# Biased attention on one core: a first group of four head pairs instead of three, bf16 loads by GpSimd, V landed in place, and the odd slot of the two-chunk pass read in two exps

## The chip, the cores and the metric

The kernel runs on one core of one Trainium2 chip. The metric is the device time of one execution in microseconds, lower is better. The engines are named as in the profile: PE (matmuls, with PEld for its weight loads), DVE (VectorE), ACT (ScalarE), POOL (GpSimd) and SP (SyncE). DMAs that SP and ACT issue go over hardware queues (q1 and q10 in the profile); DMAs that POOL issues go over the software queue q0, and these can cast f32 to bf16 on the way.

## The reference

```python
def setup_inputs():
    batch, n_heads, seq_len, head_dim = 4, 8, 1024, 64
    # q, k, v: (4, 8, 1024, 64) float32, 0.1 * normal; bias: (1, 1, 1024, 1024) float32, 0.1 * normal

def reference(q, k, v, bias):
    scale = 1.0 / np.sqrt(head_dim)
    scores = scale * np.matmul(q, k.transpose(0, 1, 3, 2)) + bias
    scores_max = np.max(scores, axis=-1, keepdims=True)
    attn = np.exp(scores - scores_max) / (np.sum(np.exp(scores - scores_max), axis=-1, keepdims=True) + 1e-8)
    return np.matmul(attn, v).astype(np.float32)
```

## The kernel before

**Tiling.** The 32 heads are taken as 16 pairs. A head's 1024 queries are 8 chunks of 128, and so are its keys. Scores are made transposed, keys on partitions, in two PSUM tiles `sx` and `sy` of three banks each (a bank is 512 f32 columns); the even "slots" use `sx`, the odd ones `sy`. The query chunks are split into three passes, `CH = {"A": (6, 2), "B": (3, 3), "C": (0, 3)}`: pass A takes chunks 6 and 7 (two banks a slot), B and C three chunks each (three banks a slot). One step is a pass, a pair and a head h, and it is two slots.

**The bias.** It is added once at the beginning of a pass, by matmuls of the bias chunk with a scaled identity (a "restart"). After that PSUM is never cleared: each step adds this head's scores and subtracts those of the head before it in the same 128-row contraction. That is what the operand tiles are for: `KA`, `KB`, `QA`, `QB` hold the two heads of a pair on the two halves of the partitions, with signs, and the lower half of `KB` and `QB` at pair r + 1 is a copy of pair r. They are rings of `RP = 9` pairs.

**Exp and AV.** ACT reads a slot with one exp (or two, where `cut_of` says so) into the bf16 ring `E` of `EB = 56` banks. Some slots leave their last bank to DVE, which makes the exp in a chain of seven instructions (`d_fixed`, `d_steps`, lines 222 to 241). The AV matmuls (`av_blocks`, line 272) take 128x128 blocks of `E` as weights and V with a column of ones, `VV` (pairs x 16 chunks x 65), as the moving operand; `evac` divides by the sum and stores.

**Transposes and copies.** Raw k and q (bf16, `kr` and `qr`) are transposed by PE (`transpose_pe`, line 147) into the PSUM tiles `xa` and `xb`, which the AV accumulators use as well. DVE copies them to `KA` and `QA`; from pair 3 on the second copies are made by DMAs on SP (lines 724, 727, 748, 752).

**Groups and order.** The pairs go in three groups, `range(0, 3)` with passes ABC, `range(3, 8)` with CAB, `range(8, 16)` with BCA, so a pass is restarted seven times. The first six slots are written out by hand (lines 288 to 482). From there a planner written in Python puts the instructions in order when the kernel is built: it holds a time for each engine (`t_act`, `t_pe`, `t_dve`), the costs `EXP`, `EXP0` and others, due times of the first loads (`raw_at`, `v_at`, `R["bias", ...]`), and picks the next fill (`pe_fill`), transposing piece (`pe_piece`), AV block (`pe_av`) or early third bank of the slots after a pass A (`pe_pre`). What it emits is fixed: each engine runs its own list in that order and waits on semaphores.

**Loads.** For the first group SP issues f32 loads into a stage inside `E` (lines 311 to 326): k and the last two chunks of q of pair 0, bias chunks 6 and 7, k and q of pairs 1 and 2, bias chunks 3 to 5, V of pair 0, the rest of q. Engines cast them: ACT and DVE pair 0, POOL (line 294) most of the others. POOL issues V of pairs 1 and 2 and bias chunks 0 to 2 with a cast on the way (lines 361 to 365), and all k, q and V of the later pairs (`load_qk`, `load_v`). A V lands in `vs` (two buffers) and `v_copy` (line 142) copies it on DVE into the 65-column layout of `VV`; the next V's load is issued with that copy.

Of the kernel before, what the change touches and what calls it, by code (L numbers as in the profile page):

```python
# [9 lines left out]
BF = mybir.dt.bfloat16  # L10
# [6 lines left out]
def kernel(  # L17
# [11 lines left out]
    nc = tc.nc  # L29
# [17 lines left out]
    raw = ctx.enter_context(tc.tile_pool(name="raw", bufs=3))  # L47
    vsp = ctx.enter_context(tc.tile_pool(name="vsp", bufs=2))
# [35 lines left out]
    groups = [(range(0, 3), "ABC"), (range(3, 8), "CAB"), (range(8, NP), "BCA")]  # L84
# [42 lines left out]
    vst = {}  # L127
# [8 lines left out]
    def load_v(pr):  # L136
        vs = vsp.tile([P, 2 * NCH, D], BF, name="vs")
        nc.gpsimd.dma_start(out=vs.rearrange("p (t c) d -> p t (c d)", t=2), in_=vf[pr])  # L138
        vst[pr] = vs

    def v_copy(pr):
        nc.vector.tensor_copy(VV[:, pr % RP, :, :D], vst.pop(pr)[:])  # L142
# [66 lines left out]
    def s_exp(s, n, pos, cut=None):  # L209
        e_pos[s] = pos  # L210
        for a, b in ((0, n),) if cut is None else ((0, cut), (cut, n)):
            read_of(s, a, b, nc.scalar.activation(E[:, (pos + a) * 512:(pos + b) * 512],  # L212
                                                  XY[s % 2][:, a * 512:b * 512], ACTF.Exp, scale=scale))
# [74 lines left out]
    with tc.manual_schedule():  # L288
# [9 lines left out]
        sk = {1: stage(1024)}  # L298
        sq = {1: stage(256)}
        sk[2], sq[2] = stage(1024), stage(256)  # L300
        sqr = {0: stage(768)}
        for c in (3, 4, 5):
            sc[c] = stage(1024)
        sv0 = stage(1024)
        sqr[1], sqr[2] = stage(768), stage(768)
# [6 lines left out]
        sp_.dma_start(out=two(sq0), in_=qf[0][:, :, 6 * D:])  # L312
# [3 lines left out]
        sp_.dma_start(out=sk[1][:, :512], in_=kf[1][:, 0])  # L316
        sp_.dma_start(out=two(sq[1]), in_=qf[1][:, :, 6 * D:])
        sp_.dma_start(out=sk[1][:, 512:], in_=kf[1][:, 1])
        sp_.dma_start(out=two(sk[2]), in_=kf[2])
        sp_.dma_start(out=two(sq[2]), in_=qf[2][:, :, 6 * D:])  # L320
        sp_.dma_start(out=two(sqr[0]), in_=qf[0][:, :, :6 * D])
        for c in (3, 4, 5):
            sp_.dma_start(out=sc[c], in_=bf_[:, c, :])
        sp_.dma_start(out=two(sv0), in_=vf[0])
        for pr in (1, 2):
            sp_.dma_start(out=two(sqr[pr]), in_=qf[pr][:, :, :6 * D])
# [15 lines left out]
        for pr in range(3):  # L342
            raws[pr, 1] = raw.tile([P, 2, NCH, D], BF, name="kr")
            raws[pr, 0] = raw.tile([P, 2, NCH, D], BF, name="qr")
# [4 lines left out]
        HK = S // 2  # L349
        kr0, qr0, kr1, qr1 = raws[0, 1], raws[0, 0], raws[1, 1], raws[1, 0]  # L350
        cast(g, btraw[:, 7, :HK], sc[7][:, :HK])
        k1 = [kr1[:, t].rearrange("p c d -> p (c d)") for t in range(2)]
        cast(g, k1[0], sk[1][:, :512])
        cast(g, k1[1], sk[1][:, 512:])
        cast(g, raws[2, 1].rearrange("p t c d -> p (t c d)"), sk[2])
        cast(g, *q_part(2, 6, 8, sq[2]))
        cast(g, *q_part(0, 0, 6, sqr[0]))
        for c in (3, 4, 5):
            cast(g, btraw[:, c, :], sc[c])
        cast(g, VV[:, 0, :, :D], sv0.rearrange("p (c d) -> p c d", d=D))  # L360
        load_v(1)
        cast(g, *q_part(1, 0, 6, sqr[1]))
        cast(g, *q_part(2, 0, 6, sqr[2]))
        load_v(2)
        g.dma_start(out=btraw[:, :3, :], in_=bf_[:, :3, :])

# [10 lines left out]
        for i in range(8):  # L377
            on(1, 0, 1, nc.tensor.matmul(XY[1][:, :512], zeros[:, :P], zeros[:, :P].unsqueeze(1).to_broadcast([P, 4, P]),
                                         start=True, stop=True, skip_group_check=True))
        cast(v_, *q_part(0, 6, 8, sq0))  # L380
        cast(nc.scalar, kr0[:, 0, :, :], sk0.rearrange("p (c d) -> p c d", d=D))

        pq = ps.tile([P, 2, P], BF, tag="xa", name="px")
        pq_ = ps.tile([P, 2, P], BF, tag="xb", name="px")
        transpose_pe(pq, qr0, 6, 2)
        for c in range(2):
            nc.tensor.transpose(pq_[:D, c, :], qr0[:, 0, 6 + c, :], ident[:])
        pk = [XY[y][:, 1024:1024 + 2 * P].bitcast(BF) for y in range(2)]
        for c in range(NCH):
            on(c // 4, 2, 3, nc.tensor.transpose(pk[c // 4][:D, c % 4 * P:(c % 4 + 1) * P], kr0[:, 0, c, :], ident[:]))  # L390
        sc_(QA[:, 0, 6 * P:], pq.rearrange("p c q -> p (c q)"), sgn[:, :1], None, op0=ALU.mult)
        nc.scalar.copy(QB[:D, 0, 6 * P:], pq_[:D].rearrange("p c q -> p (c q)"))
        on(0, 2, 3, nc.scalar.copy(KA[:D, 0, :HK], pk[0][:D]))
        on(1, 2, 3, v_.tensor_copy(KA[:D, 0, HK:], pk[1][:D]))
        v_.tensor_copy(btraw[:, 6, :5 * P], sc[6][:, :5 * P])
        nc.scalar.copy(btraw[:, 6, 5 * P:], sc[6][:, 5 * P:])
# [19 lines left out]


        first, last = [False] * 3 + [True] + [False] * 3 + [True], [False] * 8
# [9 lines left out]
        for c in range(NCH):  # L428
            nc.tensor.transpose(pk0[D:, c, :], kr0[:, 1, c, :], ident[:])
# [537 lines left out]
```

## Time and profile before

| what | value |
|---|---|
| median of 3 runs | 242.34 us (241.03 to 243.36) |
| profiled execution | 242.21 us, span 240.3 us, granted clock 1.000 |
| PE busy | 224.1 us (93%) |
| ACT busy | 224.3 us (93%) |
| DVE busy | 217.0 us (90%) |
| POOL busy | 43.4 us (18%) |
| DVE copies of V (`v_copy`, line 142) | 15, 6.2 us in sum |
| DMA written | 33.47 MB, of it 11.54 MB by the software queue |

The span runs from the first instruction to the last; the run's time has 1.9 us more around it. Busy times of ACT overlap from one exp to the next, so an exp's row is longer than the distance to the next start. A slice is a fortieth of the span, 6.0 us, and its digit the busy share in tenths. In the list of waits, what stands behind the arrow is the instruction or DMA whose semaphore came last. "issue" is time in which the engine waited for nothing that the profile shows.

### The profile page before, as it was taken

The numbers are of one execution on the slowest core, as the hardware profiler recorded it, in microseconds if no ns is written. First come the engines' busy times: TensorE is split into PE (matmuls) and PEld (weight loads), VectorE is DVE, ScalarE is ACT, GpSimd is POOL, SyncE is SP. The second block draws the span as 40 slices with busy tenths as digits, with TensorE's granted clock in tenths as the row PEclk, the third lists the DMA queues.
The fourth block names the chain that finished last, engine by engine and source line by source line (L and its number), as shares of the span: only waits on it lengthen the run. The fifth ranks groups of instructions, "written<-read, shape, count | busy, mean of one in ns | idle before, by whom it ended". The sixth has DMA issues, their size and how long they took to land.

```text
span 240.3 us, 9405 instructions
## 1 busy us (share of the span) xinstructions
PE 224.1 (93%) x4010; PEld 188.1 (78%) x4010; DVE 217.0 (90%) x455; ACT 224.3 (93%) x250; POOL 43.4 (18%) x67
## 2 busy tenths in 40 slices
PE   7997899999999999999999999999999888999982
PEld 3776588888888998878778778887877677987982
DVE  3773799999999899989999999999999999999983
ACT  4586999999999999999999999999999999999992
POOL 4468822243411311111322000000000000000000
PEclk9999999999999999999999999999999999999999
DMA  7994999999999692787699862321111111020112
GB/s 234 379 391 101 175 205 217 252 220 259 243 255 183 101 177 81 125 184 137 136 183 214 200 139 59 90 67 34 35 50 55 33 59 44 8 62 25 50 43 67
DMA packets 32041, 33.47 MB, mean 139 GB/s; under 512 B 2560, under 2 KB 27008, under 8 KB 32000
## 3 DMA queue, kind: packets, MB, share of 16 engines
q0 software_dynamic: 11296, 11.54, 32.1%
q1 hardware_dynamic: 20560, 21.08, 28.3%
q8 instruction: 31, 0.51, 0.9%
q10 hardware_dynamic: 144, 0.26, 0.4%
q14 instruction: 10, 0.08, 0.1%
HBM read 29.36 MB, written 8.39 MB: 157 GB/s over the span
## 4 chain that ended last, share of the span: by engine, by line
PE 44%; ACT 25%; DMA 13%; issue 9%; DVE 7%; SPq 1%; POOL 0%; ACTq 0%; DVEq 0%
ACT E L212 25%; PE sx L183 14%; PE po L272 13%; PE sy L183 13%; DMA vs<-in_v_dram 5%; DMA E<-in_v_dram 4%; PE px L147 4%; DMA E<-in_q_dram 3%; DVE ob L284 1%; DVE KA L733 1%; DMA out_dram<-ob 1%; DVE scr L239 1%; DVE scr L223 1%; DVE scr L238 1%; DVE QA L739 1%
## 5 line engine op out<-in xcount | busy, mean ns | idle before, releaser
L212 ACT ACTIVATE E<-sy 128x1024 bf16<-128x1024 f32 (+2 forms) x126 | 123.9, 1023 | 0.7 <-PE sy L183 0.4
L212 ACT ACTIVATE E<-sx 128x1024 bf16<-128x1024 f32 (+2 forms) x111 | 118.0, 1084 | 4.6 <-PE sx L183 2.4
L272 PE MATMUL po<-VV,E 128*128 128x65 bf16 x1896 | 81.8, 194 | 1.6 <-DVE ob L284 1.0
L272 PEld LDWEIGHTS <-E 128*128 128x128 bf16 x1896 | 74.8, 98 | 8.1 <-DVE ob L284 1.5
L183 PEld LDWEIGHTS <-KA 128*128 128x128 bf16 x648 | 47.8, 97 | 12.7 <-issue 4.2
L183 PEld LDWEIGHTS <-KB 128*128 128x128 bf16 x600 | 44.4, 97 | 13.3 <-issue 6.1
L183 PE MATMUL sx<-QB,KB 128*128 128x128 bf16 (+2 forms) x300 | 35.0, 251 | 2.9 <-ACT E L212 2.5
L183 PE MATMUL sy<-QA,KA 128*128 128x128 bf16 (+2 forms) x312 | 35.9, 252 | 1.5 <-ACT E L212 1.1
L183 PE MATMUL sx<-QA,KA 128*128 128x128 bf16 (+2 forms) x312 | 35.6, 252 | 1.7 <-ACT E L212 1.4
L183 PE MATMUL sy<-QB,KB 128*128 128x128 bf16 (+2 forms) x300 | 35.0, 251 | 1.2 <-ACT E L212 0.9
L240 DVE SCALAR_TENSOR_TENSOR e<-scr 128x512 bf16<-128x512 f32 x38 | 26.2, 690 | 1.0
L284 DVE TENSOR_TENSOR ob<-po,rs 128x384 f32<-128x384 f32 (+2 forms) x49 | 24.8, 506 | 2.1 <-DMA out_dram<-ob 0.4
L237 DVE SCALAR_TENSOR_TENSOR scr<-scr 128x512 f32<-128x512 f32 x38 | 26.0, 684 | 0.0
L239 DVE SCALAR_TENSOR_TENSOR scr<-scr 128x512 f32<-128x512 f32 x38 | 26.0, 684 | 0.0
L238 DVE SCALAR_TENSOR_TENSOR scr<-scr 128x512 f32<-128x512 f32 x38 | 25.9, 683 | 0.0
L223 DVE TENSOR_SCALAR scr<-sx 128x512 int32<-128x512 f32 x25 | 17.1, 685 | 0.3 <-PE sx L183 0.2
L236 DVE TENSOR_SCALAR scr<-scr 128x512 int16<-128x512 int16 x38 | 16.0, 422 | 0.0
L235 DVE TENSOR_SCALAR scr<-scr 128x512 f32<-128x512 uint16 x38 | 15.9, 419 | 0.0
L138 POOL DMA_DIRECT2D vs<-in_v_dram x15 | 11.4, 757 | 23.9 <-DVE VV L142 19.9
L133 POOL DMA_DIRECT2D qr<-in_q_dram x13 | 9.4, 724 | 30.1 <-PE px L147 28.3
L283 DVE RECIPROCAL rs<-po 128x6 f32<-128x6 f32 (+2 forms) x49 | 9.0, 184 | 6.3 <-PE po L272 6.2
L132 POOL DMA_DIRECT2D kr<-in_k_dram x13 | 9.4, 722 | 24.1 <-PE px L147 23.9
(79 smaller groups left out, 180.6 us busy)
## 6 DMA issues: line engine op xcount, KB each, us to landing
out_dram<-ob SPq DMA_DIRECT2D x32, 192.0 KB, 2.8
vs<-in_v_dram POOLq DMA_DIRECT2D x15, 256.0 KB, 6.0
KB<-KA SPq DMA_DIRECT2D x26, 128.0 KB, 5.7
kr<-in_k_dram POOLq DMA_DIRECT2D x13, 256.0 KB, 8.0
qr<-in_q_dram POOLq DMA_DIRECT2D x13, 256.0 KB, 7.4
QB<-qn SPq DMA_DIRECT2D x24, 128.0 KB, 5.2
E<-in_bias_dram SPq DMA_DIRECT2D x5, 512.0 KB, 7.2
out_dram<-ob SPq DMA_DIRECT2D x15, 128.0 KB, 1.9
```

Of the source, the lines that this page charges most:

```text
L138: nc.gpsimd.dma_start(out=vs.rearrange("p (t c) d -> p t (c d)", t=2), in_=vf[pr])
L183: m = nc.tensor.matmul(o, lhsT, rhs, start=restart and i == 0, stop=i == len(todo) - 1 or not restart, skip_group_check=True)
L212: read_of(s, a, b, nc.scalar.activation(E[:, (pos + a) * 512:(pos + b) * 512], XY[s % 2][:, a * 512:b * 512], ACTF.Exp, scale=scale))
L223: i = nc.vector.tensor_scalar(ys[ch % 2].bitcast(I32), XY[s % 2][:, b * 512:(b + 1) * 512], scale * LOG2E * 65536.0, 127.0 * 65536.0, op0= ...
L235: (350, lambda: v_.tensor_scalar(sf, lo, G / 65536.0, None, op0=ALU.mult)),
L236: (350, lambda: v_.tensor_scalar(sp, hi, 0.0, 128.0, op0=ALU.max, op1=ALU.mult)),
L237: (610, lambda: v_.scalar_tensor_tensor(sb, sf, U2, sf, op0=ALU.add, op1=ALU.mult)),
L238: (610, lambda: v_.scalar_tensor_tensor(y, sf, U1, sf, op0=ALU.add, op1=ALU.mult)),
L239: (610, lambda: v_.scalar_tensor_tensor(sb, sb, V2, sp.bitcast(BF), op0=ALU.add, op1=ALU.mult)),
L240: (720, lambda: v_.scalar_tensor_tensor(e[:], y, V1, sb, op0=ALU.add, op1=ALU.mult)),
L272: nc.tensor.matmul(po[u][:, h - hs[0], c - c0, :], e_block(s, col), VV[:, pr % RP, h * NCH + kc, :], start=first, stop=left[u] == 0, skip_ ...
L284: nc.vector.tensor_tensor(ob[:], acc[:, :, :, :D], rs[:].to_broadcast([P, nh, W, D]), op=ALU.mult)
```

## The change

Four things are changed together, and the planner's constants with them.

1. The groups become `range(0, 4)`, `range(4, 9)` and `range(9, 16)`. The pools `vsp` is dropped and `raw` has four buffers. The fourth pair gets direct DVE copies to `KB` and `QB` as pairs 0 to 2 have.
2. SP keeps the f32 loads of pair 0's k, bias chunks 6 and 7, and pair 1's k and last q chunks. All other loads of the first group are issued by POOL as bf16, behind two small casts on POOL that wait for bias 7 and for the second half of pair 1's k. q of pair 0 moves to ACT's queue. The head's order of casts, transposes and copies is rewritten.
3. V is loaded by two DMAs straight into `VV`, in runs of 64 elements; `v_copy` is gone. `load_v` is issued when the pair's k and q have been, and the ring has room.
4. In pass A the odd slot is read by two exps, one a bank. At the step from A to the next pass, the third banks of both new slots are read first, then the others.

```diff
-    raw = ctx.enter_context(tc.tile_pool(name="raw", bufs=3))
-    vsp = ctx.enter_context(tc.tile_pool(name="vsp", bufs=2))
+    raw = ctx.enter_context(tc.tile_pool(name="raw", bufs=4))
...
-    groups = [(range(0, 3), "ABC"), (range(3, 8), "CAB"), (range(8, NP), "BCA")]
+    groups = [(range(0, 4), "ABC"), (range(4, 9), "CAB"), (range(9, NP), "BCA")]
...
     def load_v(pr):
-        vs = vsp.tile([P, 2 * NCH, D], BF, name="vs")
-        nc.gpsimd.dma_start(out=vs.rearrange("p (t c) d -> p t (c d)", t=2), in_=vf[pr])
-        vst[pr] = vs
-
-    def v_copy(pr):
-        nc.vector.tensor_copy(VV[:, pr % RP, :, :D], vst.pop(pr)[:])
+        for t in range(2):
+            nc.gpsimd.dma_start(out=VV[:, pr % RP, t * NCH:(t + 1) * NCH, :D],
+                                in_=vf[pr][:, t].rearrange("p (c d) -> p c d", d=D))
...
         nc.scalar.dma_start(out=sk0, in_=kf[0][:, 0])
-        sp_.dma_start(out=two(sq0), in_=qf[0][:, :, 6 * D:])
+        nc.scalar.dma_start(out=two(sq0), in_=qf[0][:, :, 6 * D:])
...
+        cast(g, btraw[:, 7, :GB], sc[7][:, :GB])
+        for pr in (2, 3):
+            if pr == 3:
+                cast(g, kr1[:, 1].rearrange("p c d -> p (c d)"), sk1[:, 512:])
+            load_q(pr, 6, 8)
+            g.dma_start(out=raws[pr, 1].rearrange("p t c d -> p t (c d)"), in_=kf[pr])
+        load_q(0, 0, 6)
+        g.dma_start(out=btraw[:, 3:6, :], in_=bf_[:, 3:6, :])
+        load_v(0)
+        for pr in (1, 2, 3):
+            load_q(pr, 0, 6)
+        for pr in (1, 2):
+            load_v(pr)
         g.dma_start(out=btraw[:, :3, :], in_=bf_[:, :3, :])
+        load_v(3)
...
+        cast(v_, kr0[:, 0, 4:], k0[1])
+        cast(nc.scalar, kr0[:, 0, :4], k0[0])
...
+        cast(v_, kr0[:, 1, 4:], k0b[1])
+        cast(nc.scalar, kr0[:, 1, :4], k0b[0])
...
+        nc.scalar.copy(btraw[:, 7, GB:HK], sc[7][:, GB:HK])
         v_.tensor_copy(btraw[:, 7, HK:], sc[7][:, HK:])
...
     def cut_of(s):
...
             if n == 3 and s // 2 + 1 in restarts:
                 return 2
+            if n == 2 and s % 2:
+                return 1
...
         def v_step():
+            nonlocal next_v, dma_t
+            if next_v < next_load and not any(units[u][1] == next_v - RP for u in range(av_u, NU)):
+                load_v(next_v)
...
         def act_pick():
+            if i in pre_slots:
+                todo = [(i, 2, 3), (i + 1, 2, 3), (i, 0, 2), (i + 1, 0, 2)]
+            else:
+                c = cut_of(i) or n
+                todo = [(i, 0, c), (i, c, n)][:1 + (c < n)]
```

The planner's due times become, in its own clock, V of pairs 0 to 3 at 22800, 28000, 30000 and 35000 ns, the bias of pass B at 21000 and of pass C at 34000, and its rule for which PE work may go ahead of a fill is rewritten (`PSL`, `PSU`, `URG`, `NEAR`).

In the order that the changed program has, there are 267 exps instead of 244, over 473 PSUM banks instead of 474; 39 DVE chains instead of 38; 32 V DMAs on POOL instead of 15, each of half a V; and SP has 105 instructions instead of 116. The numbers of PE's fills and transposes stay.

## The prediction

> **What bounds the kernel now.** I read the page's busy table first, then its slices, then ACT's exps in order of time, then the loads. The busy table says three engines share the bound, and the slices say where they are not full:
>
> ```profile
> PE 224.1 (93%) x4010; PEld 188.1 (78%) x4010; DVE 217.0 (90%) x455; ACT 224.3 (93%) x250; POOL 43.4 (18%) x67
> ...
> ACT  4586999999999999999999999999999999999992
> POOL 4468822243411311111322000000000000000000
> ...
> DMA  7994999999999692787699862321111111020112
> ```
>
> ACT is short of 9 in the first four slices (24 us) and in the last. So I measure ACT's exps against their own pace, from start to start, because the durations overlap:
>
> ```profile
> 14.40 1.03 ACT L212 ACTIVATE E<-sy 128x1024 bf16<-128x1024 f32 x1
> 15.42 1.02 ACT L212 ACTIVATE E<-sx 128x1024 bf16<-128x1024 f32 x1
> 16.34 1.02 ACT L212 ACTIVATE E<-sy 128x1024 bf16<-128x1024 f32 x1
> 17.74 1.02 ACT L212 ACTIVATE E<-sx 128x1024 bf16<-128x1024 f32 x1 [0.38 <-issue]
> 18.66 1.02 ACT L212 ACTIVATE E<-sy 128x1024 bf16<-128x1024 f32 x1
> 20.92 1.02 ACT L212 ACTIVATE E<-sx 128x1024 bf16<-128x1024 f32 x1 [1.24 <-issue]
> 21.99 1.02 ACT L212 ACTIVATE E<-sy 128x1024 bf16<-128x1024 f32 x1
> 23.86 1.45 ACT L212 ACTIVATE E<-sx 128x1536 bf16<-128x1536 f32 x1 [0.85 <-PE sx L183]
> ```
>
> Two banks take 0.92 us from start to start (15.42 to 16.34); later in the timeline three take 1.33 (31.11 to 32.44) and one 0.48 (225.70 to 226.18). That is 0.427 us a bank and 0.062 an instruction, the constants `EXP` and `EXP0` of the planner. Before has 244 exps over 474 banks: 202.4 + 15.1 = 217.5 us. The span is then 7.1 us ahead of the first exp, 217.5 of work, 4.7 behind the last exp (its row ends 0.1 later than the pace has it), and 11.0 of holes. Laying the starts against the pace places the holes: 2.65 up to 16 us, 2.93 from 16.3 to 26.5 (the last two bracketed waits above and 16.34 to 17.74), 5.35 after that: 1.26 in 40 to 60 us, 0.84 at 83 to 86, 0.74 at 98.9, the rest in pieces below 0.55. Outside the start ACT is the bound, and only holes and ACT's own work can move the end.
>
> What ended the hole at 19 us is seen on PE:
>
> ```profile
> 19.24 0.47 PE L183 MATMUL sx<-ident,btraw 128*128 128x128 bf16 x4 [1.14 <-POOL btraw L294]
> ```
>
> The second pass's bias was landed as f32 and cast on POOL (four casts of 1.04 us with the V behind them). ACT had run out of banks of pass A.
>
> **Part 1: four pairs in the first group, bf16 loads.** The head (to the sixth slot) keeps its length or wins a little. Bias chunk 6 now goes first on SP and shares the engines with k of pair 0; q of pair 0 follows on ACT's queue and comes some 0.5 us later, but PE now transposes k first, so the first exp stays near 6.9 instead of 7.1. Against that ACT takes a half cast of k and 448 columns of bias 7 (about 0.4 and 0.5 us by the rows of 0.62 for 512 and 0.51 for 384), in a gap that is 1.08 us long today. Slot 4 then waits for the DVE copies of pair 1 as it does now: 13.3 against 13.50. I take -0.2, between -0.5 and +0.5.
>
> From slot 6 (15.4 us) pass A now has ten more slots instead of six. They take 5 x 0.916 + 5 x 0.978 = 9.5 us, so that pass B is wanted at 25.0 rather than 21.2. The bias of B comes as the sixth DMA on POOL. POOL's first load starts behind the small cast that waits for bias 7 (8.5 us in the timeline); the first bytes follow 1.4 us after an issue (the V issued at 21.06 shows traffic at 22.5). What lies up to and with the bias is 0.13 + 0.52 + 0.13 + 0.52 + 0.39 + 1.57 MB of f32. The rate is in this window:
>
> ```profile
> q0 software_dynamic: 796, 0.77, 116.6%
> ```
>
> It is 32 to 36 us: 0.77 MB written in 4 us is 0.385 MB of f32 read a us. With a break at the cast for k of pair 1, the third DMA starts at 13.1 and the bias ends 2.62 / 0.385 = 6.8 us later, at 19.9, visible at about 20.8. PE's order asks for it before it fills slot 14, at about 22.3. So the 2.93 us of holes go to about 0.3: -2.6. If the loads are 2 us slower than that, half of it is gone.
>
> The ten POOL casts that go (3.1 + 2.4 + 1.0 + 1.0 us and smaller) free an engine that is 18% busy: nothing.
>
> **Part 2: V landed in place.** The 15 copies of V on DVE go, 6.2 us. The fourth pair's direct copies (2 x 0.69, 0.54, 0.56, 2 x 0.27, 0.29 and the split QA), and a 39th DVE chain of 4.3 us (0.685 + 0.42 + 0.42 + 3 x 0.684 + 0.69) take that and 1.5 us more: DVE stays near 218. What ACT sees is one bank fewer, -0.43.
>
> In exchange each V is two DMAs whose runs are 128 B at a step of 130 B: 2 x 1024 packets where there were 256. No row shows such a packet. Two rows price it, the smallest packets and the largest:
>
> ```profile
> q1 hardware_dynamic: 144, 0.07, 10.3%
> ...
> q1 hardware_dynamic: 255, 0.69, 96.6%
> ```
>
> The first is 238 to 240.3 us, 128 rows of 512 B with 16 completions: 0.103 x 2.3 x 16 / 128 = 30 ns, 26 with the completions counted. The second is 4 to 6 us: 30.9 us of engine time for 225 packets of 3.07 kB, 137 ns. A line through 28 and 137 gives 17 ns for the 256 B read, 2.2 us a V over 16 engines; no gain below 512 B at all gives 28 ns, 3.6 us. I take 2.3, near the line, since the price falls with the bytes in every row there is.
>
> PE's order tells what lateness costs. The AV of pair 0 stands before fill 15, of pair 1 before fill 21, of pair 2 before fill 24, of pair 3 before fill 26, and everything behind it on PE, the next fill first, waits with it; on the pace above these are wanted at 23.3, 29.5, 32.7 and 36.3 us. At 2.2 a V the queue behind the bias (V0, 1.18 MB of q, V1, V2, 1.57 MB of bias C, V3) lands V3 at 19.9 + 4 x 2.2 + 3.1 + 4.1 and 0.8 allowed for its completion = 36.7, 0.4 late; each 0.1 on the price adds 0.4, so 2.3 makes it 0.8 late and 3.6 makes it 6.0. I take +0.8, between 0 (the V before it lands early enough to be read by then) and 6.0. Later Vs are asked for a group ahead.
>
> [...]
>
> **Part 3: the odd slot of pass A in two exps.** ACT goes from 244 to 267 exps over 473 banks: 23 x 0.062 - 0.427 = +1.0 us of work, spread over the A passes (0.94 of it behind slot 6). What it buys is an earlier first bank for PE. In the last pass A (210 us on) holes sum to 0.1, so there is nothing to buy; in the middle one it can take most of the 0.84 at 83 to 86, and with the new order of exps at the joint of A and B most of the 0.74: -1.25 for both. The last slot's first bank is also read 0.4 us sooner, which moves eight AV matmuls ahead of the last exp: -0.1.
>
> In 40 to 60 us PE is the one that is late (the chain of waits there is PE alone): it pays off AVs that waited for V. Passes B and C are now 96 banks instead of 72; a bank takes ACT 0.42 and PE 0.22 of fill and 0.12 of AV, so PE has 0.08 x 24 = 1.9 us more to spare, against 8 more banks of owed AV (1.0) and the fourth pair's transposes (0.5): -0.35.
>
> **Sum.** -0.2 - 2.6 + 0.8 + 0.94 - 1.25 - 0.1 - 0.35 = -2.76 us. The profiled execution took 242.21 (span 240.3 and 1.9 around it), the median of three is 242.34; the three spread over 1%, so 1% is about what a measurement can tell from no change. On the median: 239.6.
>
> **Rivals.** First, slower: V's small packets decide on POOL. Issuing takes POOL 566 ns for the bias and 757 for a V:
>
> ```profile
> L138 POOL DMA_DIRECT2D vs<-in_v_dram x15 | 11.4, 757 | 23.9 <-DVE VV L142 19.9
> ...
> L365 POOL DMA_DIRECT2D btraw<-in_bias_dram x1 | 0.6, 566 | 0.0
> ```
>
> The bias has 128 packets, a V 256, so 1.5 ns a packet and 1.9 us for 1024 if the difference counts; 3.0 us if the whole 757 scales. POOL has issued what lies ahead of V0 by 13.8 us (8.7 + six loads of 0.6 to 0.75 and the cast); then come eight V DMAs, three q (2.2) and bias C (0.6), and the last V lands 4.0 after its issue: 20.6 + 8 x the price. At 1.9 that is 35.8, in time; at 3.0 it is 44.6, 8.3 late where my sum has 0.8: 247.1. It decides from 2.4 us a DMA (or 3.0 us of engine time a V), where 3.5 us of stall eat the gain. For it: no data in the trace has runs below 512 B. Against: from 30 us on POOL is below 50% in every slice, so it can only bite in the first 40 us.
>
> Second, no change: the start gains, and PE gives it back. ACT reaches B 2.6 us sooner, but PE still owes the AV of 32 banks at 0.122 us, 3.9 us, plus transposes of five pairs; if that shows as holes in 26 to 60 us, +2 to +2.5: 241.9. For it is the PE chain at 30 to 57 us; against it, the ring of 56 banks lets ACT run ahead.
>
> Third, more gain: the later holes shrink to half by the planner's other new rules, and V is never late: another -0.8 - 1.5, 237.2.
>
> **How the numbers follow.** Forecast 0.50, within 238.0 to 241.0; first rival 0.23; second 0.13; third 0.14. The range reaches from the third rival's lower side, 236.8, to 246.0, which holds the first rival where engine time sets it (239.6 + 6.0 - 0.8 = 244.8). Faster than 239.9: 0.31 of the forecast and the third rival, 0.45. Within 1%: 0.19 of the forecast, 0.11 of the second, 0.02 of the first, 0.32. Slower: 0.23.
>
> **What would show it.** First exp before 7.3 us; ACT without a gap over 0.5 us between 15 and 25; the first three-bank exps near 25; the bias's landing before 22. POOL's row for a V: below 2 us right, above 2.3 wrong. PE waiting on a V's DMA for more than 1 us in sum makes the prediction wrong, and so do ACT holes over 6 us behind 26 us.

## The result, and the profile after

The changed kernel took 244.10 us (median of 17 runs, 243.39 to 249.15) where the kernel before took 240.93 (17 runs, 240.53 to 243.36): 1.3% slower, ratio 1.0129 with a 95% interval of 1.0099 to 1.0159. The forecast was 239.6. That was a gain of 2.8 us counted from 242.34, the median of the three runs known then; the 17 runs put the kernel before 1.4 us lower. Medians are over all runs, ratios leave out those that the chip disturbed, so the two can differ by some tenths of a per cent.

The page of the changed kernel, its lines of busy time and slices (the profiled execution took 244.06, span 242.1):

```profile
PE 225.4 (93%) x4009; PEld 190.2 (79%) x4009; DVE 219.0 (90%) x456; ACT 225.2 (93%) x274; POOL 56.3 (23%) x81
...
ACT  2568999999999889999999999999999999999993
...
DMA  6799999999999999512974995431112111111112
```

ACT is fuller than before in the fourth slice (8 for 6), but its first slice holds 2 where it held 4, and slices 14 and 15 (79 to 91 us) dip to 8. ACT's exps in order of time (start, duration, in brackets the wait), first two of the kernel before, then those of the changed kernel:

```profile
7.09 0.60 ACT L414 ACTIVATE E<-sx 128x512 bf16<-128x512 f32 x1 [0.69 <-PE sx L410]
...
13.50 1.02 ACT L212 ACTIVATE E<-sx 128x1024 bf16<-128x1024 f32 x1
```

```profile
9.76 0.60 ACT L401 ACTIVATE E<-sx 128x512 bf16<-128x512 f32 x1 [1.61 <-PE sx L397]
...
13.29 1.58 ACT L401 ACTIVATE E<-sx 128x512 bf16<-128x512 f32 x3 [1.69 <-PE sx L388]
...
17.20 1.02 ACT L206 ACTIVATE E<-sx 128x1024 bf16<-128x1024 f32 x1
...
22.06 1.02 ACT L206 ACTIVATE E<-sx 128x1024 bf16<-128x1024 f32 x1 [0.50 <-PE sx L178]
22.98 1.08 ACT L206 ACTIVATE E<-sy 128x512 bf16<-128x512 f32 x2
23.94 1.04 ACT L206 ACTIVATE E<-sx 128x1024 bf16<-128x1024 f32 x1
```

The first exp is at 9.76 instead of 7.09, slot 4 (the first line with L206) at 17.20 instead of 13.50. Behind it the waits of 0.85 to 1.24 us that the kernel before had at 19 to 24 us are down to 0.50. Laid against ACT's pace (0.427 us a bank, 0.062 an instruction), the spans come apart as follows (a hole is counted to the row of exps that it follows); the last column is run 13 of the experiments below, whose profiled execution took 238.91 us and was the shortest of its runs (median 239.84).

| us | before | changed | mended head, no cut |
|---|---|---|---|
| ahead of the first exp | 7.09 | 9.76 | 6.96 |
| ACT's exps, by pace | 217.53 | 218.52 | 217.47 |
| holes up to 16 us | 2.65 | 3.53 | 3.14 |
| holes 16 to 26.5 | 2.93 | 1.07 | 0.65 |
| holes 26.5 to 60 | 1.84 | 1.69 | 2.26 |
| holes 60 to 100 | 1.83 | 2.77 | 1.37 |
| holes behind 100 | 1.68 | 0.80 | 1.06 |
| behind the last exp | 4.75 | 3.96 | 4.19 |
| span | 240.3 | 242.1 | 237.1 |

Each column is one execution. That of the kernel before took 242.21, 1.3 us over its median, so the columns show 1.8 of the 3.2 us between the medians. In them the loss lies in the first 10 us (+2.7), in the holes up to 16 us and in those from 60 to 100 us (+0.9 each), and ACT's own work is +1.0; the stretch that the change was forecast to mend is mended (-1.9), and 1.7 us are gained behind 100 us and behind the last exp.

**The head.** Two casts of the timeline before, the same two in the changed kernel, and the changed kernel's DMA queues, first in 3 to 6 us, then in 3 to 4 us (packets, MB, share of 16 engines):

```profile
3.58 0.62 ACT L292 CAST kr<-E 128x512 bf16<-128x512 f32 x1 [0.88 <-DMA E<-in_k_dram]
...
3.84 0.29 DVE L294 CAST qr<-E 128x256 bf16<-128x256 f32 x1 [1.65 <-DMA E<-in_q_dram]
```

```profile
5.81 0.41 ACT L286 CAST kr<-E 128x256 bf16<-128x256 f32 x1 [2.65 <-DMA E<-in_k_dram]
...
6.99 0.29 DVE L288 CAST qr<-E 128x256 bf16<-128x256 f32 x1 [0.88 <-DMA E<-in_q_dram]
```

```profile
q1 hardware_dynamic: 281, 0.76, 68.7%
...
q10 hardware_dynamic: 373, 0.35, 33.5%
```

```profile
q1 hardware_dynamic: 56, 0.23, 64.9%
q10 hardware_dynamic: 57, 0.12, 29.9%
```

The first k is cast at 5.81 instead of 3.58, q at 6.99 instead of 3.84. With q moved to ACT's queue (q10), bias chunk 6 is the first thing on SP's queue (q1); a row of it is 4 KB, rows of k and q are 2 KB and 512 B. In these 3 us its packets, 2.7 KB in the mean, took two thirds of the engines, those of q10, 0.9 KB in the mean, one third. From 3 to 4 us q10 moves only rows of k (2.1 KB in the mean, so no q among them) and q1 only bias: 57 packets beside 56. The two queues moved nearly as many packets each, and the bias's are twice as long. In the kernel before, q10 had moved its 0.26 MB of k by 3 us, and SP's first load was the small one of q.

PE then waits 2.10 us for that cast, and is slow when it resumes. The changed kernel's transposes of k; the same work in run 1 of the experiments, where it follows PE's warm-up matmuls without a wait; and in run 2, which has 12 warm-ups:

```profile
6.27 0.64 PE L371 MATMUL sx<-ident,kr 128*64 128x128 bf16 x4 [2.10 <-ACT kr L286]
6.70 0.63 PE L371 MATMUL sy<-ident,kr 128*64 128x128 bf16 x4
```

```profile
1.00 3.17 PE L362 MATMUL sy<-zeros 128*128 128x512 bf16 x7 [1.00 <-DVE warm L309]
4.16 0.64 PE L371 MATMUL sx<-ident,kr 128*64 128x128 bf16 x4
```

```profile
5.73 0.41 PE L371 MATMUL sx<-ident,kr 128*64 128x128 bf16 x4 [0.56 <-ACT kr L286]
5.98 0.39 PE L371 MATMUL sy<-ident,kr 128*64 128x128 bf16 x4
```

Four matmuls take 0.64 us instead of 0.41, and eight 1.06 instead of 0.63 until about 12 us. The wait is not what made PE slow: run 1 has the same 0.64 without it. In these timelines PE starts at the slow pace (the warm-ups are 0.43 us apart) and leaves it later: in run 2 at 3.9 us, in the middle of its warm-ups, in the kernel before at 4.9, in run 1 at 5.6, and in the changed kernel, whose PE ran out of work at 4.2 us, at 13.0. The page's row of granted clock shows no slice below 9, but the trace's record of that clock begins at just these times, and what lies ahead of it is drawn as full (1.00 in every stretch up to 13 us of the changed kernel).

**V and POOL.** From the pages, the software queue before, and the same queue and POOL's row for V in the changed kernel:

```profile
q0 software_dynamic: 11296, 11.54, 32.1%
```

```profile
q0 software_dynamic: 42272, 13.50, 52.8%
...
L136 POOL DMA_DIRECT2D VV<-in_v_dram x32 | 28.5, 892 | 22.2 <-PE po L266 11.4
```

Issuing half a V takes POOL 0.89 us. The queue has 42272 packets where it had 11296, and 52.8% instead of 32.1%. No PE instruction waits for a V.

### The profile page after: what moved, and what is told of

Its sections match the earlier page's. It is cut to its first block, busy times and chain, and to the rows that moved or that the text cites. A ratio compares the mean times of both kernels' runs of the same rounds, so it can differ in the third digit from the quotient of the medians.

```text
span 242.1 us, 9428 instructions
## 1 busy us (share of the span) xinstructions
PE 225.4 (93%) x4009; PEld 190.2 (79%) x4009; DVE 219.0 (90%) x456; ACT 225.2 (93%) x274; POOL 56.3 (23%) x81
## 3 DMA queue, kind: packets, MB, share of 16 engines
q0 software_dynamic: 42272, 13.50, 52.8%
## 4 chain that ended last, share of the span: by engine, by line
PE 57%; DVE 25%; ACT 9%; issue 5%; DMA 2%; ACTq 0%; DVEq 0%
PE po L266 18%; PE sx L178 15%; PE sy L178 15%; ACT E L206 8%; PE px L142 6%; DVE scr L217 4%; DVE e L234 3%; DVE scr L233 3%; DVE ob L278 3%; DVE scr L232 2%; DVE scr L231 2%; DMA E<-in_k_dram 2%; DVE scr L229 2%; DVE scr L230 2%; DVE rs L277 1%
## 5 line engine op out<-in xcount | busy, mean ns | idle before, releaser
L206 ACT ACTIVATE E<-sy 128x512 bf16<-128x512 f32 (+2 forms) x139 | 124.7, 955 | 1.3 <-PE sy L178 1.3
L206 ACT ACTIVATE E<-sx 128x1024 bf16<-128x1024 f32 (+2 forms) x120 | 121.9, 1048 | 2.8 <-PE sx L178 2.1
L266 PE MATMUL po<-VV,E 128*128 128x65 bf16 x1892 | 83.6, 194 | 2.3 <-issue 1.5
L266 PEld LDWEIGHTS <-E 128*128 128x128 bf16 x1892 | 75.9, 98 | 9.5 <-issue 2.8
L136 POOL DMA_DIRECT2D VV<-in_v_dram x32 | 28.5, 892 | 22.2 <-PE po L266 11.4
L233 DVE SCALAR_TENSOR_TENSOR scr<-scr 128x512 f32<-128x512 f32 x39 | 26.6, 683 | 0.0
L231 DVE SCALAR_TENSOR_TENSOR scr<-scr 128x512 f32<-128x512 f32 x39 | 26.6, 681 | 0.0
L232 DVE SCALAR_TENSOR_TENSOR scr<-scr 128x512 f32<-128x512 f32 x39 | 26.6, 681 | 0.0
L229 DVE TENSOR_SCALAR scr<-scr 128x512 f32<-128x512 uint16 x39 | 17.1, 438 | 0.0
L130 POOL DMA_DIRECT2D kr<-in_k_dram x12 | 8.5, 709 | 33.2 <-PE px L142 32.5
L217 DVE TENSOR_SCALAR scr<-sx 128x512 int32<-128x512 f32 x21 | 14.4, 684 | 1.2 <-ACT E L206 1.1
L217 DVE TENSOR_SCALAR scr<-sy 128x512 int32<-128x512 f32 x18 | 12.3, 682 | 0.5 <-PE sy L178 0.3
```

The costliest lines, as they stand in the source:

```text
L136: nc.gpsimd.dma_start(out=VV[:, pr % RP, t * NCH:(t + 1) * NCH, :D], in_=vf[pr][:, t].rearrange("p (c d) -> p c d", d=D))
L206: read_of(s, lo, hi, nc.scalar.activation(E[:, at:at + (hi - lo) * 512], XY[s % 2][:, lo * 512:hi * 512], ACTF.Exp, scale=scale))
L217: i = nc.vector.tensor_scalar(ys[ch % 2].bitcast(I32), XY[s % 2][:, b * 512:(b + 1) * 512], scale * LOG2E * 65536.0, 127.0 * 65536.0, op0= ...
L229: (350, lambda: v_.tensor_scalar(sf, lo, G / 65536.0, None, op0=ALU.mult)),
L231: (610, lambda: v_.scalar_tensor_tensor(sb, sf, U2, sf, op0=ALU.add, op1=ALU.mult)),
L232: (610, lambda: v_.scalar_tensor_tensor(y, sf, U1, sf, op0=ALU.add, op1=ALU.mult)),
```

## The experiments

Sixteen kernels were run. The kernel before took 241.03, 241.08, 240.82 and 241.03 us beside them (runs 1 to 4, 5 to 8, 9 to 12, 13 to 16).

| run | median us | ratio to before, interval |
|---|---|---|
| 1 changed, q of pair 0 on SP | 242.55 | 1.0045 (1.0010 to 1.0081) |
| 2 changed, 12 warm-ups | 243.49 | 1.0101 (1.0072 to 1.0131) |
| 3 before, q of pair 0 on ACT's queue | 244.22 | 1.0131 (1.0103 to 1.0160) |
| 4 before, V in place | 245.28 | 1.0198 (1.0133 to 1.0263) |
| 5 changed, V staged | 246.20 | 1.0179 (1.0126 to 1.0232) |
| 6 as 5, q on SP | 243.44 | 1.0070 (1.0038 to 1.0101) |
| 7 before, with the cut of pass A | 240.39 | 0.9964 (0.9945 to 0.9982) |
| 8 changed, no cut | 244.60 | 1.0081 (1.0046 to 1.0115) |
| 9 mended head: q on SP, k cast on DVE | 241.21 | 1.0001 (0.9962 to 1.0040) |
| 10 as 9, V loaded twice | 258.00 | 1.0581 (1.0479 to 1.0684) |
| 11 as 9, second V in rows | 250.98 | 1.0363 (1.0266 to 1.0459) |
| 12 as 9, V staged | 240.73 | 1.0002 (0.9967 to 1.0038) |
| 13 as 9, no cut | 239.84 | 0.9962 (0.9935 to 0.9988) |
| 14 as 9, V in half runs | 245.24 | 1.0181 (1.0108 to 1.0254) |
| 15 as 12, no cut | 242.46 | 1.0065 (1.0046 to 1.0083) |
| 16 as 12, early DVE chains | 240.42 | 0.9967 (0.9930 to 1.0004) |

### The head

**Run 1, q of pair 0 on SP's queue again.**

```diff
-        nc.scalar.dma_start(out=two(sq0), in_=qf[0][:, :, 6 * D:])
+        sp_.dma_start(out=two(sq0), in_=qf[0][:, :, 6 * D:])
```

> The changed kernel with one line put back: q of pair 0 is issued by SP, first in its queue, as before. Theory (head): the load of k of pair 0 on ACT's queue lost its share of the DMA engines to the bias, whose packets are twice as long and now stand first on SP. With the short packets of q back in front, k lands near 3.6 us instead of 5.8, the first exp starts at 7.0 to 7.5 instead of 9.76, slot 4 near 14.2 instead of 17.20, and the time falls by 2.5 to 3.5 us to 240.6 to 241.6. Rival (V's small packets set the loss, by loading the DMA engines after 20 us): the head gains, the later holes take it back, and the time stays above 243.

242.55 us, between the theory's 240.6 to 241.6 and the rival's 243. The k cast is at 3.70 and the first exp at 6.98: the order of two DMAs is worth 2.8 us at the first exp, 2.9 at slot 4 (14.28), and 0.84 points of the 1.29 in the ratio.

**Run 2, longer warm-up.** `for i in range(7)` becomes `range(12)` in front of the first transposes.

> The changed kernel with 12 warm-up matmuls instead of 7, so that PE is busy until about 6.2 us and is not idle for 2.1 us before the first transposes. Theory (a late k, and a PE that runs at half pace after that idle time): k still lands at 5.8, but the eight first transposes take 0.7 instead of 1.07 us and the eight matmuls of the bias 0.7 instead of 1.06; the first exp comes at 9.0 to 9.3 and slot 4 at 15.8 to 16.3; the time falls by 0.8 to 1.5 us, to 242.6 to 243.3. If the idle time does not set PE's pace, rows and time stay as they are, or come 0.2 us later.

243.49 us, just over the theory's 242.6 to 243.3. PE's idle stretch shrinks from 2.10 to 0.56 us, and its matmuls are at the fast pace when k arrives, as the lines above show. That the idle time itself set the pace, as the theory had it, is not what they show: run 1 was as slow without it. k's cast came at 5.27 here, not at 5.8, so 0.5 of the 1.4 us won at slot 4 (15.81) are k's. From k's cast to slot 4 it is 10.54 us instead of 11.39, and 10.58 in run 1: the slow pace costs 0.8 us up to slot 4, and the late k 2.1 of the 2.9 that run 1 wins there. The slow pace is the smaller part of the head's loss, and the interval of this run overlaps that of the changed kernel. (The change also leaves out one of the eight warm-up matmuls, which the list of the change does not name; run 1, with seven, is at the fast pace at 5.6 us where the kernel before is at 4.9.)

**Run 3, the kernel before with q on ACT's queue**, the edit of run 1 turned round, `sp_` to `nc.scalar`.

> The kernel before with one line of the change: q of pair 0 goes to ACT's queue, so that bias chunk 6 stands first on SP. Theory (head): k of pair 0 lands at 5.5 to 6 us instead of 3.58, the first exp comes 1.8 to 2.7 us later, and the time rises by 1.8 to 2.7 us, to about 243. Rival (the order of these loads does not matter, the loss came from V and the added exps): the time stays within 0.7 us of 240.9.

244.22 us, slower by 1.3% and by more than the 2.7 us expected. Two lines of its timeline:

```profile
5.30 0.62 ACT L292 CAST kr<-E 128x512 bf16<-128x512 f32 x1 [2.13 <-DMA E<-in_k_dram]
...
17.23 1.02 ACT L212 ACTIVATE E<-sx 128x1024 bf16<-128x1024 f32 x1
```

Slot 4 moves from 13.50 to 17.23, the 3.7 us of the whole change. This one line, with no other part of the change, costs as much as the whole change; the rest of the change, taken together, then gains nothing.

**Run 9, the head mended.** Run 1, and head 1's k of pair 0 cast by DVE in one instruction, as the kernel before has it:

```diff
-        cast(v_, kr0[:, 1, 4:], k0b[1])
-        cast(nc.scalar, kr0[:, 1, :4], k0b[0])
+        cast(v_, kr0[:, 1], sk0b.rearrange("p (c d) -> p c d", d=D))
```

> The changed kernel with q of pair 0 first on SP's queue again and, besides, both halves of head 1's k of pair 0 cast by DVE in one instruction, as in the kernel before, instead of the first half by ACT behind its first two exps. With q0 on SP alone the third exp began at 10.00 us where the kernel before has 9.26, and slot 4 at 14.28 where it has 13.50; the chain there ran from ACT's cast at 7.95 to PE's transposes at 8.41 (7.61 before). Theory A (the rewritten head is a second loss beside the late bytes): third exp near 9.2, slot 4 at 13.4 to 13.7, time 0.6 to 1.0 us under the 242.55 of the q0 edit alone, so 241.5 to 242.0. Rival B (what the head gains is given back by stalls of PE at 60 to 90 us): slot 4 as early, but the time stays at 242.2 to 242.9.

241.21 us and a ratio of 1.0001: theory A's 241.5 to 242.0, and a little more. The second cause is seen in two timelines, first run 1's, then that of run 13, which has this mended head:

```profile
7.95 0.41 ACT L286 CAST kr<-E 128x256 bf16<-128x256 f32 x1
```

```profile
7.59 0.63 PE L426 MATMUL px<-ident,kr 128*64 128x128 bf16 x8
```

In run 1 ACT casts half of k behind its first two exps, and PE's transposes can start only at 8.41. Cast by DVE they start at 7.59, and slot 4 comes at 13.41 instead of 14.28. With both edits the changed kernel is level with the one before.

### V's packets

**Run 4, the kernel before with V in place**: `load_v` as in the change, `v_copy` gone, the next V issued where the ring has room.

> The kernel before with V of pairs 1 to 15 landed in place by two DMAs each, in runs of 128 B, and without the DVE copies; the planner takes a V as ready 1 us after its slot on the queue. Theory (head): V costs the DMA engines 2.0 to 2.6 us each, no AV waits for it, DVE gets 6 us back: within 1 us of before, 240 to 241.9. Rival (V's packets set the loss): the engines are overloaded from 25 to 90 us, k, q and the copies to KB and QB come late, PE waits, and the time rises by 2.5 us or more.

245.28 us, on the rival's side. Its holes from 26 to 60 us sum to 4.7 instead of 1.8. The largest, on PE and on ACT:

```profile
35.05 0.64 PE L143 MATMUL px<-ident,kr 128*64 128x128 bf16 x16 [0.92 <-DMA kr<-in_k_dram]
```

```profile
36.27 1.51 ACT L208 ACTIVATE E<-sx 128x1024 bf16<-128x1024 f32 x2 [1.21 <-PE sx L179]
```

It is k of later pairs that comes late (2.4 us of PE in three waits), not V. All of these loads stand in POOL's one queue (q0), and the author's reading is that a V that takes longer delayed what was behind it. That the changed kernel stands it better because its first group is a pair longer and leaves these loads more time is likely, but was not tried alone.

**Run 5, the changed kernel with V staged**, **run 6, the same with q on SP**, and **run 12, the same with the mended head**:

```diff
-        for t in range(2):
-            nc.gpsimd.dma_start(out=VV[:, pr % RP, t * NCH:(t + 1) * NCH, :D], ...)
+        vs = vsp.tile([P, 2 * NCH, D], BF, name="vs")
+        nc.gpsimd.dma_start(out=vs.rearrange("p (t c) d -> p t (c d)", t=2), in_=vf[pr])
+        vst[pr] = vs
...
+    def v_copy(pr):
+        nc.vector.tensor_copy(VV[:, pr % RP, :, :D], vst.pop(pr)[:])
```

`vsp` has three buffers here, and the planner's steps and due times for V's copies are put back with it. The planner makes two DVE chains fewer, since DVE has V's copies: 475 banks and 219.38 us of exps.

> The changed kernel with V put back on the old way: one DMA a pair into a staging tile (three buffers), a DVE copy into the 65-column layout. The head stays late. Theory (head plus V's packets): the DMA engines' load after 20 us falls to that of before, the gaps of PE that no semaphore explains (0.55 at 81.4 and 0.98 at 88.3 us) are gone, as is most of the excess of holes in 80 to 100 us; DVE gives 6 us back, which costs one DVE chain or less. Time 244.1 - 1.5 to 2.5 = 241.6 to 242.6. Rival (those gaps belong to the planner's new order, not to the DMA load): the gaps stay and the time does not fall, 244 or more, since DVE has more to do.

> Both parts put back: q of pair 0 first on SP, and V staged and copied by DVE. What is left of the change is the group of four pairs with bf16 loads, the order of the head and the two exps for the odd slot. Theory (head plus V's packets are the whole loss): first exp near 7.0, holes after 26 us of 4 to 5 us, and 238.0 to 239.5, below before. Rival (the added exps or the group of four cost as well): 240.5 or more.

> q0 on SP, the k cast on DVE, and V staged and copied by DVE as in the kernel before: what is left of the change is the group of four pairs with bf16 loads, the order of the head and the two exps of pass A. With q0 on SP and V staged the run took 243.44, its head had 5.06 us of holes to 16 us, and PE ran at half pace from 11 to 14 us behind an idle stretch of 0.95 us. Theory A (the head's order carries the rest of the loss): holes to 16 us fall to 2.5 to 3.5 and the time to 240.8 to 242.0. Rival B: the staged V's copies and the two DVE chains fewer hold it at 242.5 or more.

246.20, 243.44 and 240.73 us. The times of runs 5 and 6 are on their rivals' side, though PE's gaps are gone as the theory had it. They gained nothing over their partners with V in place (244.10, 242.55); ACT's 0.86 us more of work are part of that, and in both the holes up to 16 us are larger, 4.60 and 5.06. PE was slow there: run 5 reached the fast pace only at 16.5 us, and in run 6 the granted clock falls to 0.50 within an idle stretch of 0.95 us ahead of 11 us and stays there to 14. So these two do not isolate V. With the mended head run 12 is level with run 9 within the intervals, its holes up to 16 us are 2.95, and its time is just under theory A's range.

**Run 10, each V loaded a second time in the same small runs** into a tile that nothing reads, and **run 11, the second load in long rows**:

```diff
+        vd = vdp.tile([P, 2 * NCH, D + 1], BF, name="vd")      # run 11: D
+        for t in range(2):
+            nc.gpsimd.dma_start(out=vd[:, t * NCH:(t + 1) * NCH, :D], in_=...)  # run 11: one DMA of whole rows
```

> As the run with q0 on SP and the k cast on DVE, and each V is loaded a second time in the same 64-element runs into a tile that nothing reads: 32,768 packets more on the software queue and 15 to 16 KB-sized issues more of POOL. No engine's program but POOL's changes. Theory A (the small packets take engine time from k and q loads and from PE's instruction fetches): PE gains gaps that no semaphore explains, ACT's holes behind 26 us grow by 2 to 5 us, time 243.5 to 247. Rival B (V's packets cost nothing once V is in time): time within 0.7 of the run with V loaded once.

> As the run before, but the second load of each V lands in contiguous runs of 512 elements per half: the same bytes again in few packets. Theory A (it is the number of packets): at most 0.6 us over the run with V loaded once, and well under the run with the small runs twice. Rival B (it is the bytes, or POOL's issues): as slow as the small runs twice, to 0.7 us.

258.00 and 250.98 us: both far over what was expected, and not for one reason. The spare tile has one buffer, so POOL stopped for each second load until the one before had landed. The list of waits of run 11:

```profile
POOL vd L140 <- DMA vd<-in_v_dram: 49.5, 13, 6.1
```

Everything behind it in POOL's queue came late. Run 10 has the same wait (45.9 us), which was not meant. So even the difference of the two, 7.0 us with 28,928 more packets, is no clean price of a packet.

**Run 14 asks the same without a spare tile**: each V in runs of 32 elements instead of 64, the same bytes, four DMAs a pair.

```diff
         for t in range(2):
-            nc.gpsimd.dma_start(out=VV[..., t * NCH:(t + 1) * NCH, :D], ...)
+            for e in (0, D // 2):
+                nc.gpsimd.dma_start(out=VV[..., t * NCH:(t + 1) * NCH, e:e + D // 2], ...)
```

> The changed kernel with the head mended, and each V loaded in runs of 32 elements instead of 64: the same bytes, no further tile and no further wait, twice V's packets (4 DMAs of 1024 for each pair instead of 2). Theory A (a small packet has a price of its own, and late loads and PE's gaps follow): software queue's share up by about 13 points from 53%, ACT's holes behind 26 us up, time 2 to 6 us over 241.21. Rival B (bytes alone count): within 0.7 us of it.

245.24 us (four runs, 243.18 to 247.51), 4.0 over run 9: theory A, though the queue's share rises by 28 points and not by 13. Its queue line, that of run 12, where V is staged, and that of the changed kernel in 21 to 24 us:

```profile
q0 software_dynamic: 75552, 13.51, 80.5%
```

```profile
q0 software_dynamic: 13344, 13.50, 35.8%
```

```profile
q0 software_dynamic: 2378, 0.50, 187.5%
```

For 33,280 packets more at the same bytes it has 194.2 us of 16 engines instead of the changed kernel's 127.8: 32 ns of recorded time a packet. From run 12 (35.8% of 241.2 us) to the changed kernel, 28,928 packets more cost 41.5 us of 16 engines, 23 ns each, or 2.6 us more for a V than staged. Recorded times of packets overlap (the last line adds up to 187.5% of the engines), so an engine was not taken for all of that time. POOL issues twice as many DMAs in run 14, so its 4.0 us are the price of packets and their issue together.

### The cut of pass A

**Run 7, the kernel before with the cut alone**, **run 8, the changed kernel without it**, **run 13, the mended head without it**, **run 15, mended head and V staged without it**:

```diff
             if n == 3 and s // 2 + 1 in restarts:
                 return 2
+            if n == 2 and s % 2:
+                return 1
```

> The kernel before with the odd slots of pass A read by two exps, and nothing else. Theory: about 20 added exps at 0.062 us are 1.2 us of ACT's work, and the holes at 83 to 86 us go (0.5 to 0.8): +0.3 to +0.8 us, 241.2 to 241.8. Rival (an earlier first bank lets PE ahead in every pass A): faster by over 0.5 us.

> The changed kernel without the rule that reads the odd slots of pass A in two exps. Theory: ACT has some 20 exps fewer, -1.2 us of work, and the holes in its A passes grow by up to 0.8: 243.3 to 244.0. Rival (the rule carries the A passes): slower than 244.6.

> The changed kernel with the head mended (q of pair 0 on SP, head 1's k cast by DVE) and without the rule that reads the odd slot of pass A in two exps: 250 exps instead of 267, 17 x 0.062 = 1.05 us less work for ACT, 473 banks. Theory A (the cut pays more than it costs, as it did alone on the kernel before, 0.7 us): 0.3 to 1.2 us slower than the 241.21 with the cut. Rival B (the cut gains only where pass A is late): 0.5 to 1.0 faster.

> Head mended, V staged and copied by DVE, no cut of pass A: of the change the group of four pairs, the bf16 loads on POOL and the mended head are left. 474 banks and 252 exps, 218.02 us of work for ACT. Theory A (part 1 gains 1 us or more in the stretch 16 to 26.5 us, as its holes fell from 2.93 to 1.07 there): 239.8 to 240.6. Rival B (holes after 26 us take it back): 240.7 to 241.8.

On the kernel before the cut gains 0.9 us by its ratio (240.39), as the rival had it, though ACT has 1.0 us more to do: the holes up to 26.5 us fall from 5.58 to 4.02, beside the one profiled execution of the kernel before, which was 1.3 us over its median. With V staged it gains 0.6 points (run 15 against run 12). With V in place it costs 0.4 to 0.5 points, about 1 us: run 9 against 13, and the changed kernel against run 8, whose median hides it as its runs scatter over 4 us. The intervals of each pair overlap a little; the two pairs agree. So run 13 went as its rival B had it, and run 15, at 242.46, was slower than both theories: neither had the cut worth more with V staged.

These runs show two things more. Without the cut, V in place gains 1.0 points over V staged (run 13 against 15, the intervals are apart); with the cut it gains nothing (run 9 against 12). And run 15, which of the change has part 1, the mended head and the new order of exps behind a pass A, is 0.65% slower than the kernel before, though its holes from 16 to 26.5 us are 0.76 us instead of 2.93. What it wins there it loses again. Where is open: its profiled execution was 1.0 us under its median.

Run 13 is the fastest of all, 239.84. Three exps of its timeline:

```profile
6.96 0.60 ACT L401 ACTIVATE E<-sx 128x512 bf16<-128x512 f32 x1 [0.65 <-PE sx L397]
...
13.41 1.02 ACT L206 ACTIVATE E<-sx 128x1024 bf16<-128x1024 f32 x1
...
25.39 0.67 ACT L206 ACTIVATE E<-sx 128x512 bf16<-128x512 f32 x1
```

The last is the start of pass B, at 25.4. The column of the first table that bears its name shows where it differs: 1.05 us less of exps, and holes of 1.37 instead of 2.77 in 60 to 100 us.

Those holes have a pattern of their own. PE in the changed kernel:

```profile
81.06 0.32 PE L266 MATMUL po<-VV,E 128*128 128x65 bf16 x5
81.93 0.51 PE L266 MATMUL po<-VV,E 128*128 128x65 bf16 x11 [0.55 <-issue]
...
88.02 0.29 PE L266 MATMUL po<-VV,E 128*128 128x65 bf16 x4
89.28 0.42 PE L266 MATMUL po<-VV,E 128*128 128x65 bf16 x8 [0.98 <-issue]
```

and the same places in run 2, which has five warm-up matmuls more:

```profile
80.98 0.67 PE L266 MATMUL po<-VV,E 128*128 128x65 bf16 x16 [0.69 <-issue]
...
86.57 0.66 PE L178 MATMUL sx<-QB,KB 128*128 128x384 bf16 x5
88.14 0.34 PE L178 MATMUL sx<-QB,KB 128*128 128x384 bf16 x1 [0.91 <-issue]
```

PE stops in the middle of a group and waits for nothing that a semaphore shows. In the changed kernel the first gap stands behind 5 of 16 AV matmuls, in run 2 ahead of all 16; the second stands behind 6 fills and 4 AVs, in run 2 behind 5 fills. Both moved five matmuls up, exactly the five that were put in. So they belong to a place in PE's instruction stream, not to the work there. From one to the other it is 125 matmuls and as many weight loads, and with six of PE's sequencer the trace has exactly 256 records (instructions that it lists). The trace also has a queue of the kind `instruction`, q8, which moved 31 packets of 16 KB, and PE's 4009 matmuls and 4009 weight loads are 31.3 times 256: one packet for about 256 records. So the author takes these packets for the fetches of PE's instructions, each a block of 256; the trace does not name the engine. In the changed kernel, the queues in 79.6 to 80.6 us, then the software queue in 86 to 88 and in 96 to 99 us:

```profile
q0 software_dynamic: 386, 0.10, 99.0%
...
q8 instruction: 1, 0.02, 5.9%
```

```profile
q0 software_dynamic: 949, 0.27, 127.7%
```

```profile
q0 software_dynamic: 15, 0.02, 6.9%
```

One fetch ran from 79.61 to 80.56 us and the next from 86.99 to 87.92, and PE resumed 1.37 us behind the end of each. They began when PE was already 184 and 212 records into the block ahead; in the quiet stretch behind 96 us a fetch began 18 records in. So the author's reading is that PE stops because its next block comes too late.

In every run that has such gaps they stand at the same place in a block of 256 records, 1.3 to 1.8 us behind the end of a fetch. They are in every run with V in place, the cut and V loaded once, and in none with V staged. With V in place and no cut, runs 8 and 13 have none and run 4 has one, of 0.49 us; in runs 8 and 13 the tightest fetch between 40 and 93 us ended 1.43 and 1.40 us ahead of its block, so they just miss a gap. Small packets alone do not decide: run 14, with twice as many, has one gap, and run 10 none. What makes a fetch begin late isn't settled.

### A version of its own

**Run 16, mended head, V staged, DVE chains from slot 10 on instead of 14** (`DMIN` 14 to 10).

> Head mended, V staged, cut kept, and DVE's exp chains allowed from slot 10 on instead of 14, which gives back one bank: 474 banks, 262 exps, 218.64 us of work for ACT, 0.74 less than the run with V staged (240.73). A version to beat the kernels. Theory A (ACT's work sets the time): 239.8 to 240.4. Rival B (an early chain makes DVE's copies late in the prologue): 240.7 or more.

240.42 us, 0.3 less than run 12 (0.8 by the ratios) at 0.74 us less of ACT's work, just over theory A's range. Runs 7, 13 and 16 are level with each other and 0.3 to 0.4% faster than the kernel before; the interval of run 16 just reaches 1.

## Why the prediction was wrong, step by step

**Where it failed.** The step was "Bias chunk 6 now goes first on SP and shares the engines with k of pair 0; q of pair 0 follows on ACT's queue and comes some 0.5 us later", and the -0.2 us made of it. The sharing was seen, but put down as costing q half a us and k nothing. In the changed kernel the bias moved 56 packets beside 57 of k from 3 to 4 us, at twice the length: k came 2.2 us later and q 3.2, slot 4 3.7 instead of -0.2. Run 3 shows that this one move is enough for the loss, run 1 that undoing it brings the first exp to 6.98, near the forecast's 6.9, and run 9 that with one cast more the changed kernel is back to level. The same step put ACT's half cast of k "in a gap that is 1.08 us long": it stands behind two exps there, and PE's transposes behind it (run 1 to run 13, 0.9 us at slot 4). That PE, out of work at 4.2 us, would stay at its slow pace to 13 us (0.8 us at slot 4) was nowhere in the sum.

**What the head does not explain.** Level is not the forecast: without the head's -0.2 the sum still had a gain of 2.6 us, and run 9, with the mended head, has none. About 1.4 us of this is part 3, which was to gain 0.4 and whose cut costs about 1 (runs 9 and 13). The rest lies in parts 1 and 2 of the sum, and its cause stays open.

**Part 1 did its work in its stretch, but the time did not follow.** Forecast -2.6 us; the holes fell from 2.93 to 1.07, and to 0.65 with the head mended. Yet run 15, part 1 with the mended head and without V in place or the cut, is slower than the kernel before by 1.6 us at its ratio. That the start gains and the rest gives it back is what the second rival said, but not where it said: the holes from 26.5 to 60 us are 1.83 in run 15 and 1.84 before. Bias B landed by 22.9 instead of 20.8, one us past the mark of 22, but with the delayed head it was wanted only at 26; in run 13 it had landed by 21.6. Pass B was forecast from 25.0, and begins at 25.4 in run 13.

**V's price was nearly right, its consequence was not.** 2.3 us a V was taken: in 21 to 24 us the queue moved 2378 packets, a V of 2048 in 2.6 us. No AV waits for a V, so the +0.8 was not seen. What small packets cost lay elsewhere: in the k of later pairs (run 4) and in gaps of PE between 60 and 100 us. Neither was in the sum, and neither was the 1.0 points that V in place gains without the cut.

**The first rival fell.** It needed 2.4 us of POOL for half a V, its lower estimate was 1.9, and it is 0.89. The kernel is slower, as this rival had it, but for another reason.

**Part 3.** ACT's work is +0.99 as forecast with the bank saved (+0.94 behind slot 6). The -1.25 bought at 80 to 100 us was not there: holes there rose from 1.61 to 2.05, and 1.8 of these stand right behind PE's two gaps. The tail gained 0.8 instead of 0.1. Holes from 40 to 60 us fell by 0.1 instead of 0.35.

**The marks.** First exp before 7.3: no, 9.76, the mark that told. ACT without a gap over 0.5 us between 15 and 25: no, 0.5 and 0.6 in the changed kernel, 0.6 in run 13. Holes over 6 us behind 26 us: no, 5.3. From slot 4 on the span gained 1.9 us between the two profiled executions (240.3 + 3.7 - 242.1), where 2.6 were forecast; against the medians, which are 3.2 us apart, it is 0.5.

## What to carry to other kernels

Two transfers that start together moved nearly as many packets each here (56 of 4 KB and 57 of 2 KB in 1 us), so moving a small first load off a queue can promote a large one that then delays what the first instruction waits for; in a head that every engine waits for, work out which packets are in flight in the first 5 us, and which exps or casts stand ahead of the one that PE needs. When a load's runs shrink, look for the price in the other loads of that queue and in gaps without a semaphore, not only at the reader of that load. A rule that buys earlier banks with more instructions has to be measured in each version: the same two lines gained 0.9 us on one schedule and lost about 1 on another. And a profile is one execution: before two are laid side by side, compare the time of each with its kernel's median.

## What was not expected of the hardware

- Two hardware queues moved nearly as many packets each, though of different size: from 3 to 4 us one moved 56 packets of 4 KB, the other 57 of 2 KB (65 and 65 in run 3), and the first had 64.9% of the engines, the second 29.9%.
- PE starts at a slow pace, four matmuls in 0.64 instead of 0.41 us, and left it 2.9 us (run 2), 3.9 us (before) and 4.6 us (run 1) behind its first matmul at 1.0 us, but 12.0 us behind it in the changed kernel, where it was idle from 4.2 to 6.3 us. The page's row of granted clock has no sign of it, since the record begins with the fast pace. The first three lie within 1.7 us of each other; the changed kernel needed 6.7 us from 6.3 on, and no run here shows why.
- PE has gaps of 0.4 to 1.2 us at fixed places of its instruction stream, each 1.3 to 1.8 us behind the end of a 16 KB packet of the queue q8. In the changed kernel the two are 256 records apart, and their packets began 184 and 212 records into the block ahead, with the software queue at 99.0% and 127.7% of 16 engines; at 6.9% one began 18 records in.
- POOL issues a DMA of 1024 packets in 0.89 us, where one of 256 took 0.76.
